# A hybrid encoder layer: the queries' 1 / rms as the sigmoid's scale in attention, in place of a product with a row from device memory

## The chip, the cores and the metric

One core of one Trainium2 chip runs the kernel. The metric is the device time of one execution in microseconds; lower is better. Engines are named as the profile names them: PE is TensorE (PEld its weight loads), DVE is VectorE, ACT is ScalarE, POOL is GpSimd, SP is SyncE, which issues the DMAs here.

## The reference

One layer for 2048 new positions of a prompt and 64 of a running stream (called samples), width 1024. The parts that bear on the change:

```python
proj = jnp.einsum("bld,de->ble", rms_norm(x, attn_norm), w_in)
x_a, g_a, u_b, q, k, v = jnp.split(proj, SPLITS, axis=-1)
q = rms_norm(q.reshape(B, L, 4, 64), q_norm) * (64 ** -0.5)
k = rms_norm(k.reshape(B, L, 4, 64), k_norm)
# stick breaking, per query and per block of keys
z = jnp.einsum("bqhd,bkhd->bhqk", q, k)
nl = jnp.where(mask, jnp.log1p(jnp.exp(z)), 0.0)
attn = jnp.where(mask, jnp.exp(z - surv), 0.0)   # surv: sums of nl from the key on
o = jnp.einsum("bhqk,bkhd->bqhd", attn, v)
# then x + concat(y_lru, y_pool, o) @ w_out, and a SwiGLU block of width 2816
```

## The kernel before

All is fp32; each matmul operand is split into a high part in the PE's rounded format and a low part (the rest), and a product is three matmuls (`mm3`: high x high, high x low, low x high).

The prompt is cut into four groups of 512 positions (`GW`, `NG`); group 0 also carries the 64 samples (`WM` = 576 columns, done in two chunks of 288). For a group, `inproj` multiplies a weight part with the normed input `hTh`/`hTl` into PSUM banks called `mm` (three of them). Queries, keys and values of group g + 1 are projected while attention of group g runs. Tokens in strings (`o0`, `o1`, `o3` in `PRM`) give the order in which the units of a group are recorded: A, G, R a part of the LRU branch, B, b pooling, X the input, P/Q a query projection of the first and of later groups, L/K of keys, V of values, the lower-case letters their later steps; m and u are the last step of queries, n and w that of keys. Then attention's units are laid between these by weights (`WT`). Then the program's scheduler sets the final order on each engine; an engine works its instructions off in that order, and SP issues DMAs in order too.

**Queries and keys before** (`QK_parts`, L329): `mm_` leaves the projection in `raw` (L308 or L310) and its square in `sq` (L335). `ev_` multiplies `sq` with `sel` on PE, which gives sums of squares per position and head, takes 1 / rms from them on DVE and POOL (L350, L351), writes that as a row into device memory (L353) and reads it back, broadcast over 64 partitions, into `rbk` (L356; for the samples L361 and L363). `fin_` multiplies `raw` by the norm's weight and by `rbk` (L368), splits the product into `hl` (ACT cast L314, DVE subtraction L315; one buffer) and stores that (queries `q_store` L320, keys `k_store` L324).

**Attention** (`att_qtile`, L648): 128 queries against up to 512 keys. Two matmuls give `z` in PSUM, ACT makes the sigmoid of -z there (L653), DVE scans it backwards into `C` (L657 for the diagonal block, L661), PE transposes `C` into `tp`, ACT and DVE split that into `aTh` (L706) and `aTl` (L707), and PE multiplies with the values into `av`; `att_out` adds the values that belong to the first term (L669, L670) and stores into `mix`. There are 160 such tiles for the prompt and 4 for the samples.

**The output projection** (`OUT`, matmuls into `mm` with `w`, `woh`, `wol`) takes `mix` in chunks of 256 positions; the first six chunks are recorded with attention of group 3 (`merge(outs, ...)`). Its weights for k < 4 lie in buffers of pool `ws`; those for k = 4 to 7 in pool `po`, which is opened after the pools of stage 1 (`px`, `pq`, `p1`, `sm`, `pl`) are closed:

```python
    s1.close()
...
    po = s2.enter_context(tc.tile_pool(name="po", bufs=1))
...
            hi = po.tile([P, 1024], F32R, name=f"woh{k}")
            lo = po.tile([P, 1024], F32R, name=f"wol{k}")
        act.copy(hi, st)
```

(L976 is the cast, L978 and L86 the subtractions; the loads of `w_out` are L969.) Pool `pa`, which holds attention's tiles, stays open until after `OUT`. The feed-forward part follows.

Of the kernel before, what the change touches and what calls it, by code (L numbers as in the profile page):

```python
# [2 lines left out]
PRM = {'accf': 2.0, 'aend': 0.0, 'alag': 15.0, 'alag0': 20.0, 'aspan': 4.0, 'att': 100.0, 'b_C': 5.0, 'b_K': 2.0, 'b_V': 2.0, 'b_aTh': 2.0, 'b_aTl': 2.0, 'b_hl': 1.0, 'b_ms': 2.0, 'b_om': 2.0, 'b_raw': 3.0, 'b_rbk': 1.0, 'b_vT': 1.0, 'b_vf': 3.0, 'b_vp': 2.0, 'b_vs': 2.0, 'b_x2': 2.0, 'b_xh': 3.0, 'b_xk': 3.0, 'b_xr': 3.0, 'b_xt': 2.0, 'cpos': 0.0, 'db': 1.0, 'ev': 0.0, 'fine': 1.0, 'ge': 0.0, 'gelb': 2.0, 'h2p': 3.0, 'lru': 100.0, 'md': 2.0, 'mhp': 0.0, 'mlast': 6.0, 'nmm': 3.0, 'nt': 100.0, 'o0': 'P0_v0_P1_p0_G0_m0_A0_L0_R0_p1_S_l0_m1_B0_n0_A1_L1_l1_G1_R1_n1_b0_B1_A2_G2_G3_A3_R2_b1_X_Q0_Q1_R3_q0_u0_K0_q1_K1_u1_k0_k1_V_w0_w1_v', 'o1': 'A0_G0_A1_R0_G1_S_A2_R1_B0_G2_A3_R2_G3_B1_X_Q0_b0_R3_Q1_K0_q0_q1_u0_V_u1_K1_k0_w0_b1_v_k1_w1', 'o3': 'A0_G0_A1_R0_B0_G1_A2_R1_b0_G2_R2_G3_B1_A3_b1_R3', 'qlo': 1.0, 'sqb': 1.0, 'stt': 0.0, 'stt0': 2.0, 'vl': 1.0, 'vpp': 0.0, 'wd0': 1.0, 'wd1': 2.0, 'wl': 300.0, 'wm': 0.0, 'wod': 6.0, 'wok': 4.0, 'wsp': 100.0, 'xpl': 6.0, 'xrp': 0.0}  # L3
# [46 lines left out]
def hybrid_layer(ctx: ExitStack, tc: tile.TileContext, x_all, x_t, w_in, w_out, w_gu, w_dn, par, gates, poolw,  # L50
# [139 lines left out]
    dve.tensor_scalar(qn8, pv("qn"), HD ** -0.5, None, ALU.mult)  # L190
# [135 lines left out]
    def QK_parts(g, which, j):  # L326

        st = {}
# [9 lines left out]
        def ev_():  # L338
            raw, sq = st["raw"], st["sq"]
            ps = ps_st(prm('stt0', 0) if g == 0 else prm('stt', 0))  # L340
            rs = sm.tile([P, 10], F32, name="rs4")
            rs2 = sm.tile([P, 10], F32, name="rs42")
            for t in range(4):
                mm(ps[:, t:8:4], sq[:, t:GW:4], sel, True, True)
            parts = [(P, 0, 8)]
            if g == 0:
                mm(ps[:NS, 8:10], sq[:, GW:WM], sel, True, True)
                parts.append((NS, 8, 10))
            for n, a, b in parts:
                dve.tensor_scalar(rs[:n, a:b], ps[:n, a:b], 1.0 / HD, EPS, ALU.mult, ALU.add)  # L350
                gp.tensor_tensor(rs2[:n, a:b], rs[:n, a:b], mhalf[:n, 0:1].to_broadcast([n, b - a]), ALU.pow)  # L351
# [14 lines left out]
        def fin_():  # L366
            raw, (rb, W) = st["raw"], st["rb"]
            dve.scalar_tensor_tensor(raw[:, :W], raw[:, :W], qn8 if which == 0 else pv("kn"), rb[:, :W],  # L368
                                     ALU.mult, ALU.mult)
            for (a, n, t0, first) in [(0, GW, g * GW, True)] + ([(GW, NS, SEQ, False)] if g == 0 else []):  # L370
                hl = qk_split(raw[:, a:a + n], n)
                if which == 0:
                    q_store(hl, n, j, qscr[g] if first else qscr_s)
                else:
                    sp.dma_start(new_k[j * P:(j + 1) * P, t0:t0 + n], raw[:, a:a + n])
                    k_store(hl, n, j, kscr[g] if first else kscr_s[:, :, PAST:])
# [270 lines left out]
    def att_qtile(q2, n, K, w, dg, carry):  # L647
# [5 lines left out]
        act.activation(om[:n, :w], z[:n, :w], AF.Sigmoid, scale=-1.0)  # L653
# [125 lines left out]
    def IN(g):  # L779
# [4 lines left out]
        if g == 0:  # L784
            qk.update({n: [QK_parts(0, w, j) for j in range(2)] for w, n in enumerate("PL")})
# [596 lines left out]
```

## Time and profile before

| what | value |
|---|---|
| median of 3 runs | 2474.62 us (2472.97 to 2485.36) |
| the profiled execution | 2475.68 us, of which the profile's span is 2473.9 us |
| PE busy | 2310.0 us, 93% |
| DVE, POOL, ACT busy | 1569.1, 1120.2, 964.4 us |
| instructions | 38503 |

Busy times are means over stages that differ: the input projection with attention, then the output projection, then the feed-forward part. What one stage waits for is read from windows, from the waits, and from the chain of work that ended last. Times in a view's rows are microseconds from the span's start unless marked ns; PE's matmuls are pipelined, so that the durations of neighbours overlap.

### The profile page before, as it was taken

What the parts mean: (1) busy time and instruction counts of PE and PEld (TensorE: products, weight loads), DVE (VectorE), ACT (ScalarE), POOL (GpSimd) and SP (SyncE); (2) the same over time, 40 slices, a digit from 0 to 9 for tenths busy, and PEclk for the clock granted to TensorE, in tenths of its full rate; (3) what the DMA queues carried; (4) which work ended last, traced back from release to release, by engine and by line L of the source; (5) the groups of instructions that cost most, each with busy time, mean ns of one, the idle gap of its engine ahead of it and who ended that gap; (6) DMA issues with size and microseconds to landing.
All of it is one profiled execution on the core that took longest, in us unless ns stands there. A gap on an engine that the chain in (4) does not pass through costs nothing.

```text
span 2473.9 us, 38503 instructions
## 1 busy us (share of the span) xinstructions
PE 2310.0 (93%) x14158; PEld 2199.7 (89%) x14158; DVE 1569.1 (63%) x2511; ACT 964.4 (39%) x1804; POOL 1120.2 (45%) x836
## 2 busy tenths in 40 slices
PE   5876889899988998889999999999999999999999
PEld 5875768778867998889999999999999999999999
DVE  4458378488778845397767677745555565545455
ACT  4435245355456523233333334333333343333331
POOL 4443013022112124376556566655556666555552
PEclk8888799999999999999999999999999999999999
DMA  7896676665745444585434337833334464333332
GB/s 259 222 230 208 195 242 198 192 208 170 228 141 185 134 127 142 166 265 164 141 115 132 121 125 241 273 118 106 120 103 128 133 214 125 109 114 113 118 105 75
DMA packets 231383, 402.33 MB, mean 163 GB/s; under 512 B 38251, under 2 KB 102618, under 8 KB 223258
## 3 DMA queue, kind: packets, MB, share of 16 engines
q1 hardware_dynamic: 231194, 399.86, 52.1%
q8 instruction: 112, 1.84, 0.3%
q14 instruction: 77, 0.63, 0.1%
HBM read 301.07 MB, written 96.54 MB: 161 GB/s over the span
## 4 chain that ended last, share of the span: by engine, by line
PE 66%; DMA 14%; DVE 10%; issue 4%; ACT 2%; SPq 2%; POOL 2%; ACTq 0%; DVEq 0%; POOLq 0%
PE gu L78 32%; PE dn L78 20%; PE mm L78 10%; DVE C L661 1%; PE av L78 1%; PE z L78 1%; DMA wk<-w 1%; PE tp L705 1%; DMA vtscr<-vT 1%; DMA vp<-vf 1%; DMA q<-qscr 1%; DVE xc L533 1%; DMA mix<-r 1%; DMA qscr<-hl 1%; DVE aTl L707 1%
## 5 line engine op out<-in xcount | busy, mean ns | idle before, releaser
L86 POOL TENSOR_TENSOR w<-x,w 128x512 fp32r<-128x512 f32 x462 | 638.8, 1396 | 508.7 <-ACT w L1108 493.1
L78 PE MATMUL dn<-ah,wd 128*128 128x352 f32 x2112 | 548.0, 324 | 6.6 <-ACT ah L1230 3.4
L78 PE MATMUL gu<-ht,w 128*128 128x352 f32 x2112 | 545.9, 323 | 7.2 <-DVE u L1185 6.8
L1108 ACT CAST w<-x 128x512 fp32r<-128x512 f32 x462 | 279.4, 619 | 520.8 <-PE gu L78 294.1
L78 PE MATMUL mm<-hTh,w 128*128 128x512 f32 (+3 forms) x1632 | 441.8, 348 | 36.4 <-DVE raw L308 18.3
L78 PE MATMUL gu<-hb,w 128*128 128x352 f32 x1584 | 416.7, 324 | 8.5 <-ACT w L1108 7.9
L1261 DVE TENSOR_TENSOR acc<-dn,acc 128x352 f32<-128x352 f32 x528 | 273.0, 522 | 217.8 <-PE dn L78 217.2
L78 PEld LDWEIGHTS dn<-ah,wd 128*128 128x128 f32 x2112 | 376.1, 189 | 9.0 <-DVE acc L1261 4.6
L78 PEld LDWEIGHTS gu<-ht,w 128*128 128x128 f32 x2112 | 375.2, 188 | 8.6 <-issue 5.9
L78 PEld LDWEIGHTS mm<-hTh,w 128*128 128x128 f32 x1632 | 296.0, 198 | 69.2 <-DVE raw L308 18.9
L78 PE MATMUL dn<-al,wd 128*128 128x352 f32 x1056 | 342.1, 324 | 3.7 <-DVE al L1231 3.7
L78 PE MATMUL gu<-lt,w 128*128 128x352 f32 x1056 | 341.4, 323 | 0.0
L78 PEld LDWEIGHTS gu<-hb,w 128*128 128x128 f32 x1584 | 283.7, 189 | 10.5 <-ACT w L1108 8.9
L78 PE MATMUL mm<-hTl,w 128*128 128x512 f32 (+3 forms) x816 | 280.2, 344 | 0.0
L78 PE MATMUL gu<-lb,w 128*128 128x352 f32 x792 | 256.7, 324 | 0.0
L86 POOL TENSOR_TENSOR wd<-x,wd 128x512 fp32r<-128x512 f32 x132 | 192.1, 1474 | 54.7 <-ACT wd L1249 54.6
L78 PEld LDWEIGHTS dn<-al,wd 128*128 128x128 f32 x1056 | 199.4, 189 | 4.9 <-DVE al L1231 4.9
L78 PEld LDWEIGHTS gu<-lt,w 128*128 128x128 f32 x1056 | 198.8, 188 | 0.0
L78 PEld LDWEIGHTS mm<-hTl,w 128*128 128x128 f32 x816 | 161.5, 198 | 14.5 <-issue 2.1
L661 DVE TENSOR_TENSOR_SCAN C<-z,C,zero 128x512 f32<-128x512 f32 (+4 forms) x148 | 160.1, 1086 | 10.9 <-ACT z L653 9.6
L1185 DVE TENSOR_TENSOR u<-gu,u 128x352 f32<-128x352 f32 x132 | 68.8, 521 | 129.1 <-PE gu L78 128.7
L78 PEld LDWEIGHTS gu<-lb,w 128*128 128x128 f32 x792 | 149.8, 189 | 0.0
(262 smaller groups left out, 3524.3 us busy)
## 6 DMA issues: line engine op xcount, KB each, us to landing
x<-in_w_gu SPq DMA_DIRECT2D x220, 256.0 KB
w<-wk SPq DMA_DIRECT2D x46, 1024.0 KB
x<-wsc SPq DMA_DIRECT2D x176, 256.0 KB
x<-in_w_dn SPq DMA_DIRECT2D x132, 256.0 KB
wsc<-x SPq DMA_DIRECT2D x88, 256.0 KB
wk<-w SPq DMA_DIRECT2D x16, 1024.0 KB
V<-vscr SPq DMA_DIRECT2D x40, 256.0 KB
K<-kscr SPq DMA_DIRECT2D x40, 256.0 KB
```

The source lines that it names most:

```text
L78: pe.matmul(out, lhsT, rhs, start=start, stop=stop)
L86: gp.tensor_tensor(out, src, hi, ALU.subtract)
L533: dve.scalar_tensor_tensor(xc[:, a:b], xa[:, s + j:s + j + b - a], pv("cw", c * 4 + j), xc[:, a:b], ALU.mult, ALU.add)
L661: dve.tensor_tensor_scan(C[:n, :w][:, ::-1], om[:n, :w][:, ::-1], zero1[:n].to_broadcast([n, w]), carry, ALU.mult, ALU.add)
L705: pe.transpose(tp[:, kt, :], at[:, kt * P:(kt + 1) * P], ident)
L707: dve.tensor_tensor(aTl[:, :nk, qq * P:(qq + 1) * P], tp[:, :nk, :], aTh[:, :nk, qq * P:(qq + 1) * P], ALU.subtract)
L1108: act.copy(w[:, 0, :], src)
L1185: add = lambda o, x, y: dve.tensor_tensor(o, x, y, ALU.add)
L1261: dve.tensor_tensor(acc[:, d, a:b], ps[:, :HT], acc[:, d, a:b], ALU.add)
```

## The change

Queries are no longer normed before they are stored. `Q_parts` splits the projection, times the norm's weight and -1/8, into `hl` right behind the evacuation (from PSUM, or from `raw` for group 0), and stores it. The 1 / rms of a query, which lies in `att_qtile` on the partition of its row, becomes the scale of the sigmoid, and the minus sign of that scale moves into the weight (`qn8`). The reciprocals stay in new tiles `qrs` of pool `p1`: two per parity of the group, one for each pair of heads. The steps m and u leave the strings `o0` and `o1` in `PRM`. Keys are done as before. The core of the diff:

```diff
@@ -187,7 +187,9 @@
     gw = p1.tile([P, 2, 4, P], F32, name="gw")
     pw = p1.tile([P, 2, P], F32, name="pw")
     qn8 = p1.tile([P, 1], F32, name="qn8")
-    dve.tensor_scalar(qn8, pv("qn"), HD ** -0.5, None, ALU.mult)
+
+    dve.tensor_scalar(qn8, pv("qn"), -HD ** -0.5, None, ALU.mult)
+    qrs = [[p1.tile([P, 10], F32, name=f"qrs{i}{j}") for j in range(2)] for i in range(2)]
     sel = p1.tile([P, 2], F32, name="sel")
     gp.memset(sel, 0.0)
     for e in range(2):
@@ -315,16 +317,55 @@
         (dve if prm("qlo", 0) else gp).tensor_tensor(hl[:, 1, :n], raw, hl[:, 0, :n], ALU.subtract)
         return hl
 
-    def q_store(hl, n, j, dst):
-        for e in range(2):
-            sp.dma_start(dst[2 * j + e], hl[e * HD:e * HD + HD, :, :n].bitcast(F32))
-
     def k_store(hl, n, j, dst):
         for e in range(2):
             sp.dma_start(dst[2 * j + e].rearrange("(a d) t -> d a t", a=2), hl[e * HD:e * HD + HD, :, :n].bitcast(F32))
 
-    def QK_parts(g, which, j):
-
+    def sums(g, sq, ps, rs2, step):
+
+        rs = sm.tile([P, 10], F32, name="rs4")
+        for t in range(4):
+            mm(ps[:, t:8:4], sq[:, t:GW:4] if step else sq[:, t * P:t * P + P], sel, True, True)
+        parts = [(P, 0, 8)]
+        if g == 0:
+            mm(ps[:NS, 8:10], sq[:, GW:WM], sel, True, True)
+            parts.append((NS, 8, 10))
+        for n, a, b in parts:
+            dve.tensor_scalar(rs[:n, a:b], ps[:n, a:b], 1.0 / HD, EPS, ALU.mult, ALU.add)
+            gp.tensor_tensor(rs2[:n, a:b], rs[:n, a:b], mhalf[:n, 0:1].to_broadcast([n, b - a]), ALU.pow)
+
+    def Q_parts(g, j):
+
+        st = {}
+
+        def mm_():
+            sq = pq.tile([P, WM], F32, name="sq", bufs=prm("b_sq", 1))
+            for ps, a, b in inproj(g, 0, j):
+                n = b - a
+                x = ps[:, :n]
+                if g == 0:
+                    x = pq.tile([P, WM], F32, name="raw", bufs=prm("b_raw", 2))[:, :n]
+                    leave(x, ps[:, :n], g, a)
+                act.activation(sq[:, a:b], x, AF.Square)
+                hl = pq.tile([P, 2, GW], F32R, name="hl", bufs=prm("b_hl", 1))[:, :, :n]
+                act.activation(hl[:, 0, :], x, AF.Copy, scale=qn8)
+                dve.scalar_tensor_tensor(hl[:, 1, :], x, qn8, hl[:, 0, :], ALU.mult, ALU.subtract)
+                m = min(b, GW) - a
+                for e in range(2):
+                    h = hl[e * HD:e * HD + HD].bitcast(F32)
+                    sp.dma_start(qscr[g][2 * j + e][:, :, a:a + m], h[:, :, :m])
+                    if m < n:
+                        sp.dma_start(qscr_s[2 * j + e], h[:, :, m:])
+            st["sq"] = sq
+
+        def ev_():
+            sums(g, st["sq"], ps_st(prm('stt0', 0) if g == 0 else prm('stt', 0)), qrs[g % 2][j], False)
+
+        return mm_, wrap("ev", ev_)
+
+    def K_parts(g, j):
+
+        which = 1
         st = {}
 
         def mm_():
@@ -336,19 +377,8 @@
             st["raw"], st["sq"] = raw, sq
 
         def ev_():
-            raw, sq = st["raw"], st["sq"]
-            ps = ps_st(prm('stt0', 0) if g == 0 else prm('stt', 0))
-            rs = sm.tile([P, 10], F32, name="rs4")
             rs2 = sm.tile([P, 10], F32, name="rs42")
-            for t in range(4):
-                mm(ps[:, t:8:4], sq[:, t:GW:4], sel, True, True)
-            parts = [(P, 0, 8)]
-            if g == 0:
-                mm(ps[:NS, 8:10], sq[:, GW:WM], sel, True, True)
-                parts.append((NS, 8, 10))
-            for n, a, b in parts:
-                dve.tensor_scalar(rs[:n, a:b], ps[:n, a:b], 1.0 / HD, EPS, ALU.mult, ALU.add)
-                gp.tensor_tensor(rs2[:n, a:b], rs[:n, a:b], mhalf[:n, 0:1].to_broadcast([n, b - a]), ALU.pow)
+            sums(g, st["sq"], ps_st(prm('stt0', 0) if g == 0 else prm('stt', 0)), rs2, True)
             row = qkrow[g][which][j]
             sp.dma_start(row.rearrange("h (p t) -> p h t", t=4), rs2[:, :8].rearrange("p (h t) -> p h t", t=4))
             rb = pq.tile([P, WM], F32, name="rbk", bufs=prm("b_rbk", 1))
@@ -365,15 +395,11 @@
 
         def fin_():
             raw, (rb, W) = st["raw"], st["rb"]
-            dve.scalar_tensor_tensor(raw[:, :W], raw[:, :W], qn8 if which == 0 else pv("kn"), rb[:, :W],
-                                     ALU.mult, ALU.mult)
+            dve.scalar_tensor_tensor(raw[:, :W], raw[:, :W], pv("kn"), rb[:, :W], ALU.mult, ALU.mult)
             for (a, n, t0, first) in [(0, GW, g * GW, True)] + ([(GW, NS, SEQ, False)] if g == 0 else []):
                 hl = qk_split(raw[:, a:a + n], n)
-                if which == 0:
-                    q_store(hl, n, j, qscr[g] if first else qscr_s)
-                else:
-                    sp.dma_start(new_k[j * P:(j + 1) * P, t0:t0 + n], raw[:, a:a + n])
-                    k_store(hl, n, j, kscr[g] if first else kscr_s[:, :, PAST:])
+                sp.dma_start(new_k[j * P:(j + 1) * P, t0:t0 + n], raw[:, a:a + n])
+                k_store(hl, n, j, kscr[g] if first else kscr_s[:, :, PAST:])
 
         def fin():
             with behind("act", "dve", "pool"):
@@ -644,13 +670,13 @@
     zero1 = pa.tile([P, 1], F32, name="zero1", bufs=1)
     gp.memset(zero1, 0.0)
 
-    def att_qtile(q2, n, K, w, dg, carry):
+    def att_qtile(q2, rs, n, K, w, dg, carry):
 
         z = psum.tile([P, GW], F32, name="z", tag="z", bufs=prm("nz", 2))
         mm(z[:n, :w], q2[:, 0, :], K[:, :w], True, False)
         mm(z[:n, :w], q2[:, 1, :], K[:, :w], False, True)
         om = z
-        act.activation(om[:n, :w], z[:n, :w], AF.Sigmoid, scale=-1.0)
+        act.activation(om[:n, :w], z[:n, :w], AF.Sigmoid, scale=rs)
         C = pa.tile([P, GW], F32, name="C", bufs=prm("b_C", 5))
         if dg:
 
@@ -698,7 +724,8 @@
                         qt = pr * 2 + qq
                         nk = 4 if c < g else qt + 1
                         dg = P if c == g else 0
-                        at, st["carry"][qt] = att_qtile(q2[:, :, qt * P:(qt + 1) * P], P, K, nk * P, dg,
+                        at, st["carry"][qt] = att_qtile(q2[:, :, qt * P:(qt + 1) * P], qrs[g % 2][h // 2][:, (h % 2) * 4 + qt:(h % 2) * 4 + qt + 1],
+                                                        P, K, nk * P, dg,
                                                         st["carry"][qt])
                         tp = ps_a()
                         for kt in range(nk):
@@ -731,7 +758,7 @@
         sp.dma_start(V[:, :2, :].bitcast(F32), vscr_s[:PAST, h, :].rearrange("(t p) e -> p t e", p=P))
         sp.dma_start(V[:NS, 2, :].bitcast(F32), vscr_s[PAST:, h, :])
         av = psum.tile([P, GW], F32, name="av", tag="av", bufs=1)
-        at, _ = att_qtile(q2[:, :, :n], n, K, w, NS, 0.0)
+        at, _ = att_qtile(q2[:, :, :n], qrs[0][h // 2][:n, 8 + h % 2:9 + h % 2], n, K, w, NS, 0.0)
         tp = ps_a()
         aTh = pa.tile([P, 4, 256], F32R, name="aTh", bufs=prm("b_aTh", 2))
         aTl = pa.tile([P, 4, 256], F32R, name="aTl", bufs=prm("b_aTl", 2))
@@ -782,9 +809,9 @@
         bp = [POOL_parts(g, j) for j in range(2)]
         qk = {}
         if g == 0:
-            qk.update({n: [QK_parts(0, w, j) for j in range(2)] for w, n in enumerate("PL")})
+            qk.update({n: [f(0, j) for j in range(2)] for f, n in ((Q_parts, "P"), (K_parts, "L"))})
         if g < NG - 1:
-            qk.update({n: [QK_parts(g + 1, w, j) for j in range(2)] for w, n in enumerate("QK")})
+            qk.update({n: [f(g + 1, j) for j in range(2)] for f, n in ((Q_parts, "Q"), (K_parts, "K"))})
         o = "o0" if g == 0 else "o3" if g == NG - 1 else "o1"
         o = PRM[o].replace("_", " ")
         for tok in o.split():
@@ -801,8 +828,8 @@
                 f = lambda: V_unit(g + 1)
             elif k == "v":
                 f = lambda: vlag.pop(0)()
-            elif k in "uwmn":
-                f = qk["QKPL"["uwmn".index(k)]][int(tok[1])][2]
+            elif k in "wn":
+                f = qk["KL"["wn".index(k)]][int(tok[1])][2]
             else:
                 f = qk[k.upper()][int(tok[1])][k in "qkpl"]
             us.append((WT[k], f, tok))

```

The order on three engines, before and in the change. Names end in buffer numbers, which differ between the two programs; `woh`, `wol` are weights of the output projection, `z`, `tp`, `av` are attention's.

PE, before, where the first `woh` matmuls stand (attention of group 3, the second of its four heads):

```order
L78 MATMUL mm<-hTh,woh_7822 128x256
L78 MATMUL mm<-hTl,woh_7822 128x256
L78 MATMUL mm<-hTh,woh_7822 128x256
L78 MATMUL mm<-hTl,woh_7822 128x256
L78 MATMUL z<-K,q_6595 128x512 x2
L705 MATMUL tp<-ident,C 128x128 x4
L78 MATMUL mm<-hTh,woh_7822 128x256
L78 MATMUL mm<-hTl,woh_7822 128x256
L78 MATMUL z<-K,q_6595 128x512 x2
L78 MATMUL mm<-hTh,wol_7823 128x256
L78 MATMUL mm<-hTh,woh_7828 128x256
L78 MATMUL mm<-hTl,woh_7828 128x256
```

These output matmuls, on `woh` as on `w`, stand between the units of attention, with half of that group's `z` still to come.

PE, in the change, the end of group 3's attention on `q` of its last head, down to the first `woh` matmul:

```order
L78 MATMUL z<-K,q_7346 128x512 x2
L732 MATMUL tp<-ident,C 128x128 x4
L78 MATMUL av<-aTl,V 128x256
L78 MATMUL av<-aTh,V 128x256
L78 MATMUL av<-aTl,V 128x256
L78 MATMUL av<-aTh,V 128x256
L78 MATMUL av<-aTl,V 128x256
L78 MATMUL av<-aTh,V 128x256
L78 MATMUL av<-aTl,V 128x256
L732 MATMUL tp<-ident,C 128x128 x4
L78 MATMUL av<-aTh,V 128x256
L78 MATMUL mm<-hTh,woh_7766 128x256
```

The two `z` at the top are the last of the group; the first `woh` matmul has moved behind them, and none stands ahead of them.

ACT, before, where `woh` is cast:

```order
L653 ACTIVATE z<-z 128x512
L976 CAST woh_7822<-stg 128x1024
L976 CAST woh_7828<-stg 128x1024
L653 ACTIVATE z<-z 128x512
L706 CAST aTh<-tp 128x4x128
L653 ACTIVATE z<-z 128x512
L706 CAST aTh<-tp 128x4x128
```

The first casts stand between sigmoids of group 3.

ACT, in the change, where the same casts stand:

```order
L679 ACTIVATE z<-z,qrs_186 128x512
L733 CAST aTh<-tp 128x4x128
L1003 CAST woh_7766<-stg 128x1024
L1003 CAST woh_7772<-stg 128x1024
L733 CAST aTh<-tp 128x4x128 x2
L1003 CAST woh_7778<-stg 128x1024
L1003 CAST woh_7784<-stg 128x1024
```

The first `woh` cast has moved behind the last sigmoid of the program, L679.

SP, before, where the queries of group 0 are loaded for attention:

```order
L687 DMA V<-vscr_61 128x4x128
L682 DMA q_1730<-qscr_65 64x1024 x2
L682 DMA q_1966<-qscr_65 64x1024 x2
L320 DMA qscr_s<-hl 128x1x64 x2
L223 DMA stg<-in_w_in 128x1024
```

The loads of the first two heads stand behind value loads and ahead of a store of sample queries.

SP, in the change, the same loads:

```order
L295 DMA xrow_104<-rs_2992 128x4
L415 DMA vscr_61<-vs 128x512
L434 DMA vp<-vf 63x256
L436 DMA vp<-in_cache_v 1x256
L708 DMA q_1722<-qscr_65 64x1024 x2
L708 DMA q_1958<-qscr_65 64x1024
L225 DMA stg<-in_w_in 128x1024
L356 DMA qscr_65<-hl 128x1x288 x2
L234 DMA wk_1_1230<-w_1225 128x2048
```

They have moved to an earlier place, ahead of the weight load `stg<-in_w_in` and of the second pair's query store.

## Rows read from the trace of the kernel before

**Rows 1.** The page: span; busy time, share of the span and instructions.
```profile
span 2473.9 us, 38503 instructions
...
PE 2310.0 (93%) x14158; PEld 2199.7 (89%) x14158; DVE 1569.1 (63%) x2511; ACT 964.4 (39%) x1804; POOL 1120.2 (45%) x836
```

**Rows 2.** Waits of PE, 0 to 200 us: in total, times, longest.
```profile
PE mm L78 <- DVE raw L308: 18.3, 2, 10.9
```

**Rows 3.** ACT in time: start, us, line, operation [idle before <-releaser].
```profile
105.40 0.78 ACT L565 ACTIVATE r<-r,sp 128x576 f32<-128x576 f32 x1
...
113.64 0.69 ACT L571 ACTIVATE sqt<-r 128x576 f32<-128x576 f32 x1
...
140.45 0.24 ACT L314 CAST hl<-raw 128x64 fp32r<-128x64 f32 x1 [9.92 <-DMA qscr<-hl]
...
175.58 0.24 ACT L314 CAST hl<-raw 128x64 fp32r<-128x64 f32 x1 [11.22 <-DMA qscr<-hl]
```

**Rows 4.** Windows: length, PE PEld DVE ACT POOL SP busy us (x instructions), PE clock, DMA.
```profile
750.00:775.80 25.80, 19.90 (x127) 16.52 (x126) 23.80 (x35) 16.59 (x28) 6.18 (x4) 0.93 0.44 138
...
775.80:800.00 24.20, 23.47 (x175) 21.29 (x174) 23.11 (x30) 16.66 (x32) 6.29 (x5) 1.00 0.63 202
...
825.00:850.00 25.00, 25.00 (x199) 24.24 (x199) 21.01 (x32) 12.86 (x27) 2.94 (x4) 1.00 0.38 110
```

**Rows 5.** One window, all instructions; then those alone that touch tile mm.
```profile
775.80:886.60 110.80, 110.00 (x856) 104.91 (x855) 94.36 (x133) 60.63 (x120) 17.02 (x19) 1.00 0.51 150
...
775.80:886.60 110.80, 65.18 (x439) 58.94 (x440) 7.66 (x19) 0.00 (x0) 1.00 0.51 150
```

**Rows 6.** ACT in time, where the first weights of the output projection are cast.
```profile
773.94 2.00 ACT L976 CAST woh<-stg 128x1024 fp32r<-128x1024 f32 x2 [0.23 <-DMA out_o_lru<-st_lru]
...
775.85 0.58 ACT L653 ACTIVATE z<-z 128x512 f32<-128x512 f32 x1
```

**Rows 7.** DVE by line, 775.8 to 886.6 us: count | busy us, mean ns | idle.
```profile
L661 DVE TENSOR_TENSOR_SCAN C<-z,C,zero 128x512 f32<-128x512 f32 (+3 forms) x40 | 47.7, 1195 | 3.5 <-ACT z L653 3.1
L707 DVE TENSOR_TENSOR aTl<-tp,aTh 128x512 fp32r<-128x512 f32 (+3 forms) x44 | 27.8, 638 | 3.7 <-ACT aTh L706 3.6
...
L657 DVE TENSOR_TENSOR_SCAN C<-z,ident 128x128 f32<-128x128 f32 x8 | 3.2, 416 | 4.2 <-ACT z L653 4.2
...
L669 DVE TENSOR_TENSOR om<-av,q 64x512 f32<-64x512 f32 x3 | 2.1, 694 | 1.9 <-PE av L78 1.9
L670 DVE TENSOR_TENSOR om<-av,om 64x512 f32<-64x512 f32 x3 | 2.0, 676 | 0.0
```

**Rows 8.** DVE in time: three rows of attention, a weight's low part, the last sum.
```profile
735.86 1.28 DVE L661 TENSOR_TENSOR_SCAN C<-z,C,zero 128x512 f32<-128x512 f32 x1
737.05 0.67 DVE L707 TENSOR_TENSOR aTl<-tp,aTh 128x512 fp32r<-128x512 f32 x1
737.63 1.27 DVE L661 TENSOR_TENSOR_SCAN C<-z,C,zero 128x512 f32<-128x512 f32 x1
...
786.43 1.20 DVE L978 TENSOR_TENSOR wol<-stg,woh 128x1024 fp32r<-128x1024 f32 x1
...
886.60 0.68 DVE L670 TENSOR_TENSOR om<-av,om 64x512 f32<-64x512 f32 x1
```

**Rows 9.** The chain that ended last, 880 to 905 us: start, length, what.
```profile
879.90 0.72 PE mm L78 x6
```

**Rows 10.** Tiles hl and rbk: duration ns min/median/max, first and last start, forms.
```profile
L314 ACT CAST hl<-raw x22: 244/619/624, 27.9 to 691.4; 128x512 fp32r<-128x512 f32 x16, 128x64 fp32r<-128x64 f32 x4, 128x256 fp32r<-128x256 f32 x2
...
L356 SPq DMA_DIRECT2D rbk<-row x32: 444/527/1408, 102.0 to 674.6; - x32
```

**Rows 11.** Waits of PE, 200 to 400 us.
```profile
PE z L78 <- DMA q<-qscr_s: 7.0, 2, 4.5
...
PE z L78 <- DMA q<-qscr: 4.8, 2, 3.2
```

**Rows 12.** The chain, 0 to 900 us: start, length, what.
```profile
123.00 17.34 DMA qscr<-hl
```

More of the change, by code (lines that the diff above doesn't have):

```diff
@@ L2 @@
 from contextlib import contextmanager
-PRM = {'accf': 2.0, 'aend': 0.0, 'alag': 15.0, 'alag0': 20.0, 'aspan': 4.0, 'att': 100.0, 'b_C': 5.0, 'b_K': 2.0, 'b_V': 2.0, 'b_aTh': 2.0, 'b_aTl': 2.0, 'b_hl': 1.0, 'b_ms': 2.0, 'b_om': 2.0, 'b_raw': 3.0, 'b_rbk': 1.0, 'b_vT': 1.0, 'b_vf': 3.0, 'b_vp': 2.0, 'b_vs': 2.0, 'b_x2': 2.0, 'b_xh': 3.0, 'b_xk': 3.0, 'b_xr': 3.0, 'b_xt': 2.0, 'cpos': 0.0, 'db': 1.0, 'ev': 0.0, 'fine': 1.0, 'ge': 0.0, 'gelb': 2.0, 'h2p': 3.0, 'lru': 100.0, 'md': 2.0, 'mhp': 0.0, 'mlast': 6.0, 'nmm': 3.0, 'nt': 100.0, 'o0': 'P0_v0_P1_p0_G0_m0_A0_L0_R0_p1_S_l0_m1_B0_n0_A1_L1_l1_G1_R1_n1_b0_B1_A2_G2_G3_A3_R2_b1_X_Q0_Q1_R3_q0_u0_K0_q1_K1_u1_k0_k1_V_w0_w1_v', 'o1': 'A0_G0_A1_R0_G1_S_A2_R1_B0_G2_A3_R2_G3_B1_X_Q0_b0_R3_Q1_K0_q0_q1_u0_V_u1_K1_k0_w0_b1_v_k1_w1', 'o3': 'A0_G0_A1_R0_B0_G1_A2_R1_b0_G2_R2_G3_B1_A3_b1_R3', 'qlo': 1.0, 'sqb': 1.0, 'stt': 0.0, 'stt0': 2.0, 'vl': 1.0, 'vpp': 0.0, 'wd0': 1.0, 'wd1': 2.0, 'wl': 300.0, 'wm': 0.0, 'wod': 6.0, 'wok': 4.0, 'wsp': 100.0, 'xpl': 6.0, 'xrp': 0.0}
+PRM = {'accf': 2.0, 'aend': 0.0, 'alag': 15.0, 'alag0': 20.0, 'aspan': 4.0, 'att': 100.0, 'b_C': 5.0, 'b_K': 2.0, 'b_V': 2.0, 'b_aTh': 2.0, 'b_aTl': 2.0, 'b_hl': 1.0, 'b_ms': 2.0, 'b_om': 2.0, 'b_raw': 3.0, 'b_rbk': 1.0, 'b_vT': 1.0, 'b_vf': 3.0, 'b_vp': 2.0, 'b_vs': 2.0, 'b_x2': 2.0, 'b_xh': 3.0, 'b_xk': 3.0, 'b_xr': 3.0, 'b_xt': 2.0, 'cpos': 0.0, 'db': 1.0, 'ev': 0.0, 'fine': 1.0, 'ge': 0.0, 'gelb': 2.0, 'h2p': 3.0, 'lru': 100.0, 'md': 2.0, 'mhp': 0.0, 'mlast': 6.0, 'nmm': 3.0, 'nt': 100.0, 'o0': 'P0_v0_P1_p0_G0_A0_L0_R0_p1_S_l0_B0_n0_A1_L1_l1_G1_R1_n1_b0_B1_A2_G2_G3_A3_R2_b1_X_Q0_Q1_R3_q0_K0_q1_K1_k0_k1_V_w0_w1_v', 'o1': 'A0_G0_A1_R0_G1_S_A2_R1_B0_G2_A3_R2_G3_B1_X_Q0_b0_R3_Q1_K0_q0_q1_V_K1_k0_w0_b1_v_k1_w1', 'o3': 'A0_G0_A1_R0_B0_G1_A2_R1_b0_G2_R2_G3_B1_A3_b1_R3', 'qlo': 1.0, 'sqb': 1.0, 'stt': 0.0, 'stt0': 2.0, 'vl': 1.0, 'vpp': 0.0, 'wd0': 1.0, 'wd1': 2.0, 'wl': 300.0, 'wm': 0.0, 'wod': 6.0, 'wok': 4.0, 'wsp': 100.0, 'xpl': 6.0, 'xrp': 0.0}
 def prm(n,d):
```

## The prediction

> **What bounds the kernel now.** I read the page first, then the busy time by windows, then the chain and the waits inside the windows that the change touches. The page [rows 1] shows TensorE busy for 2310.0 of 2473.9 us. The feed-forward part, which begins behind the output projection, is TensorE's, and the change has nothing in it. What can move is the first 900 us. Two stretches matter there.
>
> The first is the start, where group 0 is projected. TensorE waits 18.3 us there for a vector operation that writes `raw` [rows 2], and ScalarE stands still twice, 9.92 and 11.22 us, in front of `hl<-raw` until a store of queries (`qscr<-hl`) has landed [rows 3]. The second is the end of attention for group 3. There the windows [rows 4] say something that a page's shares hide: from 775.80 us on, TensorE is full (25.00 of 25.00 us in the last of these windows), since 439 of its matmuls up to 886.60 us are not attention at all but the output projection [rows 5], laid between the attention units. VectorE has 21 to 23 us of each window there. So in that stretch attention, whose pace VectorE sets, runs under a TensorE that has other work for every gap.
>
> **What lets the output projection in.** Its weights for k = 4 to 7 (`woh`, `wol`) lie in pool `po`, which takes the memory that `s1.close()` gives back. The trace shows the price of that: ScalarE's first `woh` cast starts at 773.94 us and waited for a store out of `st_lru`, a tile of `s1` that has nothing to do with weights [rows 6]. The last reader of anything in `s1` opens the gate.
>
> The change puts `qrs` in `p1`, which is in `s1`, and lets every sigmoid of attention read it. The last reader is then the last sigmoid of group 3. The order of instructions agrees: ScalarE's `woh` casts stand behind the last sigmoid, and TensorE's `woh` matmuls behind the last `z`. **This is the main term.**
>
> **The tail, worked out.** From 775.80 us both kernels have the same TensorE work left: attention, and 439 recorded output matmuls.
> - Attention without company is VectorE's: 47.7 + 27.8 + 3.2 + 2.1 + 2.0 = 82.8 us [rows 7]. Lower bound: where VectorE runs these back to back, one tile takes 1.77 us from scan to scan (735.86 to 737.63 us), while scan and subtraction are recorded with 1.28 + 0.67 = 1.95 us [rows 8]; 82.8 x 1.77 / 1.95 = 75 us. Upper bound: VectorE was busy 23.11 of 24.20 us in the first window [rows 4], so 82.8 / 0.955 = 86.7 us. I take 82.8, which lies between and near the window that is most like it.
> - Behind the last sigmoid VectorE still has a scan, a subtraction and the two sums into `om`: 1.2 + 0.6 + 0.7 + 0.7 = 3.2 us (means of [rows 7]). So the last sigmoid is at about 775.8 + 82.8 - 3.2 = 855.4 us, and the gate opens there.
> - From the first `woh` cast to the end of the last `wol` took 786.43 + 1.20 - 773.94 = 13.7 us [rows 6, 8], since two staging buffers serve four loads. The same again: all weights are there at 869.1 us. In between TensorE has attention's last products and 15 output matmuls (the order shows 6 and 9 of them among the last units).
> - The other 424 follow. Six of them in a row took 0.72 us, 0.12 us each [rows 9]: 50.9 us. End: 869.1 + 50.9 = 920.0 us.
> - Before, the same work was done when the last attention operation ran at 886.60 us [rows 8]. The tail costs **+33 us**, between +26 and +37 by the bounds.
>
> Nothing gives this back later: after that point the output projection ran on TensorE alone already.
>
> **The start, worked out.** The change removes, for each of two pairs of heads in group 0, a row store, two broadcasts of 512 and the three for the 64 sample tokens; for six pairs in later groups, a store and two broadcasts: 30 DMAs less. Splitting at 288 columns adds 4 stores. One such issue takes 0.53 us of SP's time [rows 10]; 26 fewer are 14 us of SP, but no wait in the rows names SP, so I count them as nothing. What counts is that queries no longer hold `raw` until a row has gone to device memory and back: the split comes right behind the evacuation, and ScalarE stands less before `hl`. The longest TensorE wait for `raw`, 10.9 us of the 18.3 [rows 2], ends just when ScalarE gets past its 9.92 us at 140.45 us [rows 3]. I take that one wait as gone: **-11 us**. What is late next there is the next store of `hl`, still one buffer, and the loads behind it. Bounds: all that TensorE waits at the start for `raw`, for queries and for the sample queries, 18.3 + 4.8 + 7.0 = 30 us [rows 2, 11], as a gain; and as a loss 17 us, the longest that a query store took on the chain [rows 12], if SP stands behind it with weights queued.
>
> **The rest, about 0.** Eight VectorE operations go, about 0.67 us each as a subtraction of that size takes [rows 8]: 5.4 us on an engine that is 63% busy [rows 1]. Six ScalarE casts of 0.62 us go [rows 10]. The 164 sigmoids now read their scale from memory; an activation of 576 with such a scale took 0.78 us, one without 0.69 us [rows 3], so 0.09 us each, 15 us of ScalarE in all. A full tile then costs ScalarE about 0.58 + 0.09 for the sigmoid [rows 6] and 0.62 for the cast [rows 10], 1.29 us, below VectorE's 1.77 us, which hides it; without that cover it is the 15 us. In groups 1 to 3 the projection's PSUM bank is now held until VectorE has taken the low part and `hl` is free; no row shows that wait; it is bounded by nothing, with three banks, and by a store's landing each time, of which the one bad case is the 17 us above. Sum 0, between -5 and +15.
>
> **Sum.** 2475.7 us (the profiled execution, span 2473.9) + 33 - 11 = 2497.7. That execution stands 1.1 us above the median of 2474.6, so the forecast for the median is **2497 us**. About 0.5%, 12 us, is what a measurement of this kernel tells from no change: slower is above 2487, faster below 2462.
>
> **The rivals.**
> - *The start gives back what the tail takes (not slower).* The place is group 0's projection. If the early split takes all of TensorE's waits there and not one, the gain is 30 us: 2475.7 + 33 - 30 - 1.1 = 2478 us, no change that can be measured. It decides from a gain of 21 us on. To come out faster it would need 45, more than the waits of these rows; with the tail at its lower bound, 26, and 5 from VectorE, 2466 us is what it gives. For it: ScalarE's 21 us of standing still are all behind query stores. Against it: `hl` is still one buffer, and DMA is what that stretch waits for.
> - *SP blocks (slower still).* In the changed order the loads of heads 0 and 1 stand right behind the stores that they read, ahead of a weight load; SP waits there for the landing. 17 us lost in place of 11 won gives 2475.7 + 33 + 17 - 1.1 = 2525 us.
> - *The clock falls in the tail (slower still).* Attention alone leaves gaps on TensorE. In the tail attention has 110.0 - 439 x 0.12 = 57 us of TensorE at full clock [rows 5, 9]. In the window of [rows 4] where TensorE had 19.90 of 25.80 us the granted clock was 0.93; at that, 57 / 0.93 = 62 us, and VectorE's 82.8 stay the longer. Only below a clock of 0.69 would TensorE set the pace; at 0.6 it takes 95 us, 12 more: 2509 us. The Trainium skill, page "TensorE: Matmul & The Clock Gate", section "A second HAM failure mode: psum-queue depth-cycling", says that short, frequent idle gaps between groups of matmuls make the clock swing between its two levels. It speaks against this change; by the rows of this case the swing was small where the gaps were alike, and by the rule it could be larger, which is this rival.
>
> **How the numbers follow.** Forecast 0.62: the order of instructions fixes the mechanism, and only sizes are open. Start gives all back 0.12; SP blocks 0.10; clock 0.10; 0.06 for the rest (0.04 of it faster). Slower by over 0.5%: 0.53 of the forecast's 0.62 (the rest of it has the start at 20 us or more), both slower rivals and 0.02 of the rest, 0.75. Faster: 0.04. Within 0.5%: the 0.21 that is left. The range from 2478 to 2516 holds the forecast with its bounds (tail 26 to 41, start 0 to 25), the clock's 2509, and leaves out the ends of the two start rivals.
>
> **What would show it.** In the profile of the changed kernel the first `woh` cast stands right behind the last sigmoid; output matmuls during attention's last 75 us are few; TensorE is clearly under 25 of 25 us there while VectorE is above 23; the output projection then runs full for some 50 us more than before past attention's end. At the start the wait of TensorE for `raw` near 131 to 142 us is gone, and the first `z` comes before 203 us. If TensorE still has `woh` matmuls between the units, or attention's last 42 tiles take over 100 us, the argument is wrong.

## The result, and the profile after

The changed kernel takes 2498.82 us (median of 5 runs, 2494.64 to 2505.64), the kernel before 2475.47 us (5 runs, 2472.97 to 2485.36): a ratio of 1.0087, 95% interval 1.006 to 1.0115. That is slower by more than the 0.5% that can be told from no change. The forecast was 2497 us. The number was met; the sum behind it was met only in part, and two of its errors cancelled. The rest of this document is mostly about that.

The page of the changed kernel, its span and busy times, which answer to [rows 1]:

```profile
span 2497.0 us, 38424 instructions
...
PE 2324.9 (93%) x14158; PEld 2203.1 (88%) x14158; DVE 1567.2 (63%) x2503; ACT 973.6 (39%) x1798; POOL 1122.1 (45%) x836
```

Busy shares say nothing here: they are the same to a point. So I read the traces by place, with milestones that both programs pass in the same order: attention's score matmuls (`z<-K,q`, two per tile, 328 in all), and the end of the output projection. The kernel before and the change were both profiled again with the experiments (runs e9_before and e7_change), and these two traces, from two chips, give the table. The traces of the first pair give -22.7, -23.2, -3.7, -5.1 and +22.6 for its first five rows.

| milestone | before, us | change, us | difference |
|---|---|---|---|
| first score matmul (group 0) | 199.2 | 176.8 | -22.4 |
| 161st (group 2, values of group 3 are projected) | 602.8 | 582.1 | -20.7 |
| 193rd (end of group 2) | 651.4 | 650.7 | -0.7 |
| 225th (group 3, near the end of its first head) | 742.4 | 742.5 | +0.1 |
| end of the output projection | 1027.4 | 1052.1 | +24.7 |
| end of the last matmul | 2461.3 | 2486.9 | +25.6 |

Three things happened: the start won 22 us, a stretch of 50 us in group 2's attention lost 20 of them, and the tail lost 25. (In the expectations below score matmuls are counted from 0 and with 40 small products of `sel` that also write `z` and come first; their 40th is the first of this table, their 200th the 161st, their 264th the 225th.)

**The start.** ScalarE's waits by cause, change, 100 to 200 us (cause, us in total, times, longest):

```profile
ACT hl L316 <- DMA kscr<-hl: 6.7, 1, 6.7
...
ACT hl L316 <- DMA kscr_s<-hl: 4.0, 1, 4.0
```

The two waits of 9.92 and 11.22 us for `qscr<-hl` [rows 3] are gone, and two waits for stores of keys are what was late next. TensorE's 10.9 us wait for `raw` [rows 2] is gone too; the other of the two, 7.4 us before, is still there with 7.5.

**The tail.** ScalarE in the changed kernel, in order of time (start, us, line, operation):

```profile
843.14 0.66 ACT L679 ACTIVATE z<-z,qrs 128x512 f32<-128x512 f32 x1 [0.56 <-PE z L78]
843.73 0.59 ACT L733 CAST aTh<-tp 128x512 fp32r<-128x512 f32 x1
844.21 2.00 ACT L1003 CAST woh<-stg 128x1024 fp32r<-128x1024 f32 x2
```

The first is the last sigmoid of the program, and the first `woh` cast stands right behind it, where before it stood at 773.94 us among the sigmoids of the group's second head [rows 6]. The chain that ended last shows the same gate, as one piece (start, length, what):

```profile
770.89 74.42 issue
845.30 0.02 POOLq L86
845.32 0.02 issue
845.34 2.40 POOL wol L86
...
851.25 1.05 ACT woh L1003
...
857.90 28.87 PE mm L78 x216
```

"issue" is time for which the profile names no wait. Here 74.42 us of it stand in POOL's queue in front of a weight's low part: POOL waits for the gate.

The busy time by windows in e9_before, from the 225th score matmul to attention's last sum (the columns are those of [rows 4]):

```profile
742.40:880.70 138.30, 131.58 (x993) 122.94 (x992) 118.46 (x167) 79.19 (x149) 24.26 (x22) 0.99 0.50 148
```

And in e7_change, from the same matmul to the end of attention, and on to the point where the same number of output matmuls had been done:

```profile
742.50:849.40 106.90, 90.76 (x568) 72.11 (x566) 100.27 (x132) 67.11 (x116) 10.83 (x5) 0.97 0.36 105
849.40:906.00 56.60, 53.40 (x428) 52.82 (x429) 19.49 (x37) 17.21 (x33) 12.65 (x17) 0.97 0.55 161
```

Attention alone is VectorE's (100.27 of 106.90 us), TensorE stands for 16 us, and 428 matmuls that used to lie in those gaps come behind it: 163.5 us in place of 138.3.

**The middle**, which I had put at nothing. From the 161st to the 177th score matmul, e9_before and then e7_change:

```profile
602.80:622.60 19.80, 19.80 (x145) 18.48 (x143) 15.40 (x17) 9.05 (x17) 0.00 (x0) 1.00 0.64 208
```

```profile
582.10:614.30 32.20, 23.81 (x144) 21.74 (x142) 16.20 (x19) 9.62 (x17) 0.00 (x0) 0.84 0.43 135
```

The same work, 145 and 144 matmuls, took 12.4 us more: 8.4 us in which TensorE stood, and 4.0 us because it was busier with the same, at a granted clock of 0.84 in place of 1.00. VectorE, in the first trace of the change, says why it stood:

```profile
590.84 0.43 DVE L411 TENSOR_TENSOR vp<-vp,vf 128x256 f32<-128x256 f32 x1 [6.54 <-DMA vp<-vf]
592.63 1.26 DVE L687 TENSOR_TENSOR_SCAN C<-z,C,zero 128x512 f32<-128x512 f32 x1
...
603.08 0.43 DVE L411 TENSOR_TENSOR vp<-vp,vf 128x256 f32<-128x256 f32 x1 [6.96 <-DMA vp<-vf]
603.42 1.28 DVE L687 TENSOR_TENSOR_SCAN C<-z,C,zero 128x512 f32<-128x512 f32 x1
```

and TensorE who waited for it:

```profile
592.96 0.55 PE L78 MATMUL av<-aTh,V 128*128 128x256 f32 x1 [4.00 <-DVE om L696]
604.76 1.22 PE L78 MATMUL z<-K,q 128*128 128x512 f32 x2 [4.21 <-DVE C L687]
```

`vp` is the values moved by one position, copied by a DMA. VectorE subtracts it in its turn, and where that turn comes before the copy has landed, the scans of attention stand behind it. In e9_before the same subtractions stand in another place, behind the low part of a query:

```profile
629.77 0.68 DVE L315 TENSOR_TENSOR hl<-raw,hl 128x512 fp32r<-128x512 f32 x1
630.37 0.76 DVE L385 TENSOR_TENSOR vp<-vp,vf 128x256 f32<-128x256 f32 x2
```

and wait for nothing.

### The profile page after: what moved, and what is told of

It reads as the page before. It is cut to its first block, busy times and chain, and to the rows that moved or that the text cites. A ratio compares the mean times of both kernels' runs of the same rounds, so it can differ in the third digit from the quotient of the medians.

```text
span 2497.0 us, 38424 instructions
## 1 busy us (share of the span) xinstructions
PE 2324.9 (93%) x14158; PEld 2203.1 (88%) x14158; DVE 1567.2 (63%) x2503; ACT 973.6 (39%) x1798; POOL 1122.1 (45%) x836
## 4 chain that ended last, share of the span: by engine, by line
PE 61%; DMA 15%; DVE 12%; issue 6%; SPq 2%; POOL 2%; ACT 2%; DVEq 0%; ACTq 0%; POOLq 0%
PE gu L78 31%; PE dn L78 19%; PE mm L78 9%; DMA vp<-vf 3%; DMA wk<-w 2%; DVE C L687 1%; DMA xk<-in_x_t 1%; DVE aTl L734 1%; DMA kscr_s<-hl 1%; PE z L78 1%; PE tp L732 1%; DMA hsc1t<-xg 1%; DMA rbk<-row 1%; PE av L78 1%; POOL w L86 1%
```

## The experiments

All ratios are to runs of the kernel before on the same chip, with 95% intervals. Runs e1 to e4, e5 to e8 and e9 to e12 were on one chip each, three in all. There the kernel before took 2467.75, 2465.65 and 2468.5 us (medians), 7 to 10 us less than in the first pair. Expectations that were reckoned from 2475 or 2499 us are therefore to be held against the ratios, not against the times.

**e1_out: the change without the gate.**

```diff
-    qrs = [[p1.tile([P, 10], F32, name=f"qrs{i}{j}") for j in range(2)] for i in range(2)]
+    qrs = [[cp.tile([P, 10], F32, name=f"qrs{i}{j}") for j in range(2)] for i in range(2)]
```

> The change with its 1 / rms tiles in the constants' pool, which stays open, and nothing else. Theory (the tail's cost is the gate of the memory that the output weights reuse): from the 264th score matmul to the end of the output projection the changed kernel takes 315.8 us (743.1 to 1058.9) against 288.1 before (748.2 to 1036.3); this 27.7 us goes, 2499 - 28 = 2471 us (2463 to 2479), and the first cast of woh comes while attention still runs. Rival (the sigmoid's scale from memory makes attention slower, or attention alone would have cost that anyway): 2493 or more.

Measured: 2472.21 us, ratio 1.0016 (1.0008 to 1.0025). The first `woh` cast is back among the sigmoids:

```profile
769.36 0.66 ACT L679 ACTIVATE z<-z,qrs 128x512 f32<-128x512 f32 x1 [0.32 <-PE z L78]
771.24 2.00 ACT L1003 CAST woh<-stg 128x1024 fp32r<-128x1024 f32 x2 [1.21 <-DMA out_o_lru<-st_lru]
773.14 0.65 ACT L679 ACTIVATE z<-z,qrs 128x512 f32<-128x512 f32 x1
```

From the 225th score matmul to the end of the output projection it takes 289.0 us, against 309.6 in e7_change and 285.0 in e9_before. The choice of a pool for 160 bytes per partition was worth 20.6 us by the traces and 0.83% by the ratios (1.0099 of e7_change less 1.0016), 20 us. I had expected all of 28 us to go; that 2471 us was met comes from the faster chip.

**e2_gate and e3_scale: the gate and the scale without the change.** The kernel before, with

```diff
+    nsc = p1.tile([P, 1], F32, name="nsc")
+    gp.memset(nsc, -1.0)
...
-        act.activation(om[:n, :w], z[:n, :w], AF.Sigmoid, scale=-1.0)
+        act.activation(om[:n, :w], z[:n, :w], AF.Sigmoid, scale=nsc[:n])
```

and in e3_scale the same with `cp` for `p1`.

> The kernel before, whose sigmoids read their scale, a constant -1, from a tile in the first stage's pool; queries are normed as before. Theory: the gate alone costs the 28 us of the tail, 2475 + 28 = 2503 us (2497 to 2511), with the start and the middle as in the kernel before. Rival (the tail's cost needs the changed queries): within 6 us of before, 2470 to 2481.

> The same constant -1 in the constants' pool: the scale is read from memory, but nothing gates the output weights. Theory: 164 sigmoids get 0.08 us longer on ScalarE, which waits for others: 2476 us (2472 to 2482). Rival (ScalarE's longer sigmoid is on the path of attention): up to 13 us more, 2488.

Measured: e2_gate 2500.14 us, ratio 1.0127 (1.0114 to 1.014); e3_scale 2479.24 us, ratio 1.0044 (1.0032 to 1.0056). In e2_gate the first `woh` cast waits for the end of attention although queries go their old way:

```profile
847.98 0.66 ACT L655 ACTIVATE z<-z,nsc 128x512 f32<-128x512 f32 x1 [0.55 <-PE z L78]
849.04 2.00 ACT L978 CAST woh<-stg 128x1024 fp32r<-128x1024 f32 x2
```

Between the two lies the gate alone, 0.83% again, 20 us where I had expected 28; e2_gate met its 2503 us because the scale's cost and the faster chip came to the same sum. The scale from memory cost 11 us where I had expected 1, near the rival's 13. The sigmoid's median went from 582 to 662 ns. That the 0.08 us of 164 sigmoids, 13 us, is on attention's path is one reading; but in this kernel the scheduler also puts about one in seven of TensorE's instructions in another order, so that the two can't be parted here.

**e4_units: where the shorter unit strings lay things.** e1_out with the strings of the kernel before, in which m and u now record nothing:

```diff
+            elif k in "um":
+                f = lambda: None
```

> As e1_out, and with the steps m and u kept in the unit strings as units that record nothing, so that the weights that lay attention and the value steps between the others are as before. The changed kernel lost 18 us against the one before between the 200th and the 248th score matmul, where VectorE stands three times, 23 us in all, for the shifted copy of the values. If that comes from where the shorter strings lay the units, it goes here: 2471 - 18 = 2453 us (2446 to 2461). If it comes from the earlier start itself or from the queries' new split, this stays with e1_out at 2471.

Measured: 2458.01 us, ratio 0.9959 (0.9945 to 0.9974), 14 us below e1_out. The size was about right and the place only in part. VectorE still stood 6.45 and 6.64 us for `vp`, the 16 score matmuls from the 161st still took 33.1 us; the gain lay in the 32 score matmuls from the 193rd on (84.7 us, in e1_out 93.6) and in the 16 ahead of those (28.4 against 35.8). So the strings cost 14 us, and the wait for the shifted copy has another cause.

**e5_first and e6_later: the change for group 0 alone, and for groups 1 to 3 alone**, without gate and with the strings of before.

```diff
+    NEWQ = (0,)
+
     def Q_parts(g, j):
+        if g not in NEWQ:
+            return K_parts(g, j, 0)
```

with `NEWQ = (1, 2, 3)` in e6_later. `K_parts(g, j, 0)` sends queries through the row in device memory as before, and the sigmoids of those groups have the constant 1.0 as their scale.

> The queries' new way for group 0 and its samples alone, groups 1 to 3 as before (a row in device memory, constant scale 1 with the minus in the weight), 1 / rms tiles in the constants' pool, unit strings of before. Theory: the start wins its 23 to 27 us (40th score matmul at 177 to 181 us, before 203.6); the middle loses nothing, since VectorE's order has the value subtraction behind the queries' low part there, as before; only 20 of 164 sigmoids read a scale; no gate. 2468 - 24 = 2444 us (2438 to 2453). Rival (the middle loses because it starts earlier, whatever the queries do there): 12 us more, 2456.

> The opposite: groups 1 to 3 the new way, group 0 and the samples as before. Theory: start as before (40th score matmul at 198 to 204 us), the value subtraction on VectorE early and waiting 12 us in two pieces for its shifted copy at the turn to group 3, 144 sigmoids with a scale from memory: 2468 + 12 + 5 = 2485 us (2474 to 2493). Rival (nothing is lost in the later groups by themselves): 2462 to 2472.

Measured: e5_first 2449.51 us, ratio 0.9929 (0.9917 to 0.9942); e6_later 2470.82 us, ratio 1.0015 (1.0005 to 1.0024). e5_first won 16 us where I had expected 24; e6_later came out where its rival said. The first score matmul is at 177.3 us in e5_first and at 201.9 us in e6_later. The stretch from the 161st score matmul, e5_first and then e6_later:

```profile
579.10:598.90 19.80, 19.80 (x145) 18.48 (x143) 15.15 (x17) 9.05 (x17) 0.00 (x0) 1.00 0.63 195
```

```profile
595.50:629.50 34.00, 26.19 (x150) 23.77 (x149) 16.93 (x20) 10.31 (x18) 0.00 (x0) 0.85 0.42 133
```

and VectorE's value subtraction there, e5_first and then e6_later:

```profile
606.66 0.75 DVE L421 TENSOR_TENSOR vp<-vp,vf 128x256 f32<-128x256 f32 x2
```

```profile
601.29 0.42 DVE L421 TENSOR_TENSOR vp<-vp,vf 128x256 f32<-128x256 f32 x1 [6.51 <-DMA vp<-vf]
614.08 0.42 DVE L421 TENSOR_TENSOR vp<-vp,vf 128x256 f32<-128x256 f32 x1 [7.30 <-DMA vp<-vf]
```

This settles which part makes the middle's loss: the later groups' queries, whose step on VectorE ahead of the subtraction is gone, and neither the early start (which e5_first has) nor the strings. It does not say that the later groups lose: e6_later as a whole came out 3.7 us above before by its ratio, where I had said 17. It wins 16 us in the 8 score matmuls ahead of group 1's first (69.9 us, in e9_before 85.5), gives 14 back at the subtraction, and the 11 us or less of the scale are in its sum.

**e7_change** is the change itself, beside these:

> The change itself on the chip of the other runs: 1.0087 of before, 2489 us (2483 to 2496), against which e5_first, e6_later, and by ratio e1_out and e4_units, are measured.

Measured: 2490.44 us, ratio 1.0099 (1.0086 to 1.0112).

**e8_first_hl2: a second buffer for `hl`** (`'b_hl': 2.0`) in e5_first.

> As e5_first with two buffers for hl instead of one. What was named as late next at the start is the next store of hl. Theory: ScalarE's remaining wait for a key store there (6.7 us at 162.5 us in the changed kernel) goes, and TensorE gets little of it: 2441 us (2433 to 2446). Rival (the key steps wait for their own rows, not for the buffer): same as e5_first within 3 us.

Measured: 2451.94 us, ratio 0.9943 (0.9931 to 0.9955): the rival. ScalarE's wait in front of `hl` is 11.2 us long there, and is for VectorE's product with the key row:

```profile
ACT hl L316 <- DVE raw L405: 11.2, 1, 11.2
```

The buffer was not what keys wait for.

**e9_before** is the kernel before, for its trace:

> The kernel before, for a trace beside those of the experiments: 2466 us (2462 to 2472), 40th score matmul at 198 to 204 us, 16 score matmuls from the 200th on in 20 us, output projection ended 829 to 834 us behind the 40th score matmul.

Measured: 2467.79 us, ratio 1.0002 (0.9993 to 1.0012); first score matmul at 199.2 us.

**e10_lag and e12_first_lag: the value subtraction one tile later**, in e4_units and in e5_first.

```diff
-            if len(lag) > prm('vl', 1):
+            if len(lag) > prm('vl', 1) + 1:
```

with `'b_vf': 4.0` and `'b_vp': 3.0`.

> As e4_units, with the values' subtraction in groups 1 to 3 recorded one token tile later (and one buffer more for vp and for vf), so that the shifted copy has landed when VectorE comes to it. Theory (VectorE's standing still for that copy is what the middle loses): the stretch of 16 score matmuls from the 200th falls from 33 to 20 to 23 us; ratio to before from 0.996 to 0.991, 2443 us (2436 to 2451). Rival (attention of group 3 would wait for its keys and values there anyway): no more than 4 us from e4_units, 2452 to 2460.

> As e5_first with the later value subtraction of e10_lag. The waits of VectorE for the shifted copy that are left in the later groups there (one of 8.4 us in group 3's turn, others in groups 1 and 2) go. Theory: a few of those us are on TensorE's path, 2444 us (2438 to 2450). Rival: none is, 2447 to 2453.

Measured: e10_lag 2460.52 us, ratio 0.9974 (0.9962 to 0.9986); e12_first_lag 2460.71 us, ratio 0.9968 (0.9957 to 0.998). Neither won anything, and e12_first_lag lost 10 us against e5_first by the ratios, outside both of its ranges. In e10_lag the edit did only a part of what it was for: in the stretch from the 161st score matmul VectorE still waited 5.88 and 2.72 us for the copy, after 6.45 and 6.64 us in e4_units. TensorE's standing in that stretch fell from 7.6 us between its matmuls in e4_units to 3.5:

```profile
576.70:606.10 29.40, 25.93 (x184) 24.31 (x183) 18.30 (x24) 11.71 (x22) 2.18 (x2) 0.94 0.48 155
```

It did 184 matmuls in 29.40 us where e4_units did 150 in 33.1. But from the 209th to the 225th score matmul it took 33.5 us where e4_units took 22.5. TensorE waits 3.4 us for `xc` of the LRU branch there, as it does in e9_before (3.6 us) and e5_first (3.4 us) and does not in e4_units. At the end of the output projection e10_lag and e4_units were both at 1019 us. In e12_first_lag VectorE waits for no copy of the values of groups 2 and 3, and the kernel is slower all the same: 12 us behind e5_first at the 161st score matmul, 17 at the end of the output projection.

So the wait for the copy is where TensorE is seen to stand, but that the whole kernel loses by it is not shown: with the waits shorter or gone no time came back. The edit also changes the order of other instructions, and what holds these kernels instead was not followed further.

**e11_early: the tiles back in `p1`**, in e5_first.

> As e5_first, with the 1 / rms tiles back in the first stage's pool p1, as the change has them; their last reader is now a sigmoid of group 0's attention. Theory (what counts is the time of the last reader of that memory, not the pool): as e5_first, 0.993 of before, 2449 us (2444 to 2454). Rival (any tile of that pool that attention reads holds the output weights back): 20 us more, 2469.

Measured: 2447.77 us, ratio 0.9916 (0.99 to 0.9932), as e5_first. ScalarE's first `woh` cast waits there, as in the kernel before, for the store of the LRU's state:

```profile
745.17 2.00 ACT L1015 CAST woh<-stg 128x1024 fp32r<-128x1024 f32 x2 [0.42 <-DMA out_o_lru<-st_lru]
```

A tile of the first stage that attention reads does no harm if its last reader is early. e5_first and e11_early are the fastest versions, 0.7 and 0.8% below the kernel before.

## Why the prediction was right or wrong

**The gate: right in mechanism.** Place, cause and order were as forecast, and e1_out, e2_gate, e3_scale and e11_early show it from four sides: without the late reader the loss goes, with the late reader alone it comes, and the pool with an early reader costs nothing.

**The tail: +33 us was too much.** From the point of equal work (775.8 us before, 770.8 us in the first trace of the change) the terms came out so:
- Attention alone to its last sum: 80.1 us (850.9 - 770.8), forecast 82.8. It lies between that and the lower bound of 75: VectorE ran scan and subtraction back to back for most of the time.
- From that sum to the start of the full run of output matmuls at 857.9 us: 7.0 us, forecast 10.5. The last sigmoid came 7.7 us ahead of the last sum and not 3.2, so the gate opened earlier, and the weights took 11.8 us from first cast to last low part, not 13.7.
- Output matmuls from there to the same count as before: 52.0 us, forecast 50.9.
- Together 139.1 us, against 111.2 before: +27.9 us, and +25.2 in the pair e7_change and e9_before. The gate alone is 20 us of it (e1_out; e3_scale to e2_gate); what is over belongs to the sigmoid's scale and to what else differs, which e1_out has too (289.0 us, before 285.0). The "tail 26 to 41" of the range counts the upper bound's 4 us twice: the sum itself ends at +37.

**The start: -11 us was half of it.** The step that failed is "I take that one wait as gone". It went, but a second one went with it. Two stalls of ScalarE had the same cause, and I counted the one whose end could be seen in a TensorE wait. The view of [rows 11] has a line that I left out, between the two that I took, the wait in front of the first score matmul for the load of keys (kernel before):

```profile
PE z L78 <- DMA K<-kscr: 6.9, 1, 6.9
```

e9_before has it with 7.1 us, and e6_later, where group 0's queries go the old way, with 6.5; in the change and in e5_first it is gone. ScalarE's second stall, 11.22 us up to 175.58 us, lies ahead of it. Behind that stall, at 189.76 us, ScalarE's cast of the keys into `hl` waited for a store of sample queries. That the stall reached TensorE by the keys is a reading of this order, and no run parts it from the rest. Busy time by windows from the first product with `sel` to the first score matmul, e9_before and then e7_change:

```profile
72.10:199.20 127.10, 103.47 (x637) 97.91 (x635) 71.38 (x153) 56.05 (x97) 53.13 (x36) 0.87 0.90 256
```

```profile
70.60:176.80 106.20, 95.73 (x644) 92.04 (x643) 72.40 (x136) 47.70 (x84) 55.43 (x36) 0.94 0.87 272
```

TensorE stood 23.6 us and then 10.5, which is 13.2 us less; and it was busy 7.7 us less with as many matmuls, at a granted clock of 0.94 after 0.87. A stall has a second price that my sum did not have: the matmuls behind it run for a while at the lower of the two levels, 1.2 in place of 2.4 GHz. In the trace of the kernel before TensorE was busy for 1.52 us from 130 to 140 us, and the granted clock of the next 10 us was 0.65, the lower level for most of them. e5_first, the start alone, is 16 us faster than before (0.7%). The rival "the start gives back what the tail takes" named a gain of 21 us as its point; the start passed it, and the kernel still came out slower, because of the next term.

**The rest: "Sum 0, between -5 and +15" was wrong.** By the table 20 us were lost between the 161st and the 193rd score matmul: 12.4 in the first 16, at the value subtraction, and 7.6 in the next 16 (28.8 us before, 36.4 in e7_change). The second piece is the shorter strings', a term that the sum did not have at all: with the strings of before it is gone (28.4 us in e4_units). For the first piece, I had looked for waits that the new query steps bring (the PSUM bank, `hl`), and not for what stood behind the old ones: the step that is taken out of VectorE's queue had kept the value subtraction far enough back for its copy to land. The order of VectorE's instructions, which was there to be read, shows it. Before, at the first two subtractions of group 3's values:

```
L707 TENSOR_TENSOR aTl<-tp,aTh 128x4x128
L315 TENSOR_TENSOR hl<-raw,hl 128x512
L385 TENSOR_TENSOR vp<-vp,vf 128x256 x2
L657 SCALAR_TENSOR_TENSOR C<-z,ident 128x128 x2
```

In the change, at the first of them:

```
L734 TENSOR_TENSOR aTl<-tp,aTh 128x2x128
L411 TENSOR_TENSOR vp<-vp,vf 128x256
L695 TENSOR_TENSOR om<-av,q_4777 64x512
L696 TENSOR_TENSOR om<-av,om 64x512
L687 SCALAR_TENSOR_TENSOR C<-z,C,zero_211 128x512
```

The query's low part is gone, and the subtraction has moved up to the end of an earlier head of attention. That this place makes the loss of the stretch rests on the waits and on e5_first and e6_later; what it costs the whole kernel stays open (e10_lag, e12_first_lag).

The scale from memory, "0.09 us each, 15 us of ScalarE in all", hidden: 0.08 us each was right; that it was hidden was not borne out, since e3_scale is 11 us slower, with the reservation made there.

**The other rivals.** SP did not block: the first score matmul came 22 us earlier. The clock in the tail kept a mean of 0.97 with TensorE at 90.76 of 106.90 us, and TensorE did not set the pace. In the middle it did fall, to 0.84, where TensorE stood twice for 4 us. The rule of the Trainium skill ("TensorE: Matmul & The Clock Gate", section "A second HAM failure mode: psum-queue depth-cycling"), that frequent short gaps make the clock swing, is borne out little by the tail. TensorE's largest wait there by cause, 750 to 950 us (cause, us in total, times, longest), is many short gaps:

```profile
PE z L78 <- DVE C L687: 9.7, 21, 0.8
```

**The sum by ratios** to before: group 0's queries -0.7% (e5_first), the later groups' +0.15% (e6_later), both together -0.4% (e4_units), with the shorter strings +0.16% (e1_out), with the gate +0.9 to 1.0% (the change). My +33 and -11 made nearly the same total as 20 for the gate, 14 for the strings and -10 for the rest. That the sum was right to 2 us is luck: its terms were off by 5 to 20.

## What to carry to other kernels

Before placing a small tile, ask who reads it last and what will be laid into that memory afterwards: 160 bytes read by the last sigmoid held the output projection's weights back by 70 us; in a pool that stays open (e1_out), or with an early last reader (e11_early), they were not held back. When a step goes out of an in-order queue, read what then moves up in that queue and whether its data is there yet; here VectorE, waiting 6.5 and 7.0 us for a copy, held up the scans behind it. Where a change has a gain in one stage and a loss in another, try it stage by stage: the queries' new way is worth 0.7% for group 0 and nothing for the later ones.

## What the runs showed that was not expected

- A TensorE stall costs more than its length: in the middle stretch 8.4 us of standing came with 4.0 us more busy time for the same matmuls, at the start 13.2 us less standing with 7.7 us less busy time.
- A sigmoid of 128x512 whose scale is a tile takes 0.66 us, with a constant 0.58 us, and the kernel with that alone was 0.44% slower, with an order of instructions that differs.
